# Two Strassen pairs in the second half of the output projection of a hybrid decoder block

## The chip, the cores and the metric

The kernel runs on one core of a Trainium2 chip. The metric is the device time of one execution in microseconds (us). A core has TensorE (PE, with its weight loads listed as PEld), VectorE (DVE), ScalarE (ACT), GpSimd (POOL) and SyncE (SP), which issues most DMA transfers here. The engines run beside each other and wait for each other by semaphores.

## What is computed

One decoder layer on 256 positions of width 2048, all in float32, and a final norm. Cut to what matters:

```python
u = rms_norm(h, norm_mix)
z = u @ w_in                      # 13060 columns, 8192 of them merge gates
gates = sigmoid(gz + b_gate)      # (256, 4, 2048)
mixed = sum(gates[:, n] * (branches[n] @ w_branch[n]) for n in range(4))
h = h + mixed @ w_out             # the output projection: 256x2048 by 2048x2048
v = rms_norm(h, norm_ffn)
h = h + (silu(v @ w_ffn_gate) * (v @ w_ffn_up)) @ w_ffn_down
return rms_norm(h, norm_final)
```

## The kernel before

Every float32 matrix product is made from three matmuls of a reduced-precision type (float32r): each operand is split into a high part, which ScalarE rounds (`act`), and a low part, which VectorE subtracts (`tt`), and high x high, high x low and low x high are added up in PSUM. One such product of a 128x128 block of the stationary side (the activations, transposed) with a 128x512 block of weights is 3 matmuls (`mm3s`).

The large projections run through `pair`: two weight column blocks of 512 columns, `wl` and `wr`, against both halves of the 256 positions, over K in steps of 256 rows, called pairs (`kp`, 8 of them for K = 2048). Four accumulators, q[t][i] (t the half of the positions, i left or right block), fill four PSUM banks for the whole loop; there is one set of them, so the next call of `pair` starts in them when the results of the call before have been read out. A direct pair has its weights in four pieces of 128x1024 altogether: `wpiece` loads two K blocks of one column block into a `raw` slot (four slots), and makes `whi` and `wlo` (four slots each). It takes 8 products, 24 matmuls.

A Strassen pair (`kp in skps`) treats the 2x2 blocks of the stationary side and the 2x2 blocks of the weights as a Winograd-Strassen product: 7 products, 21 matmuls. It needs sums of the weight blocks (`s_weights`: four additions, then high and low parts of the four blocks and of three of the sums) and sums of the stationary blocks (`s_sums`: four subtractions or additions of 128x128, high and low part). Four of its products go into four PSUM banks of their own, p1, p5, p7, p6, which gather over all Strassen pairs of the call, three into q. After the last Strassen pair these banks are joined by ScalarE and VectorE into an SBUF tile `u`, which whoever called `pair` adds to q's results. In the kernel before the gates use Strassen for pairs 0, 3 and 6, the FFN for up to four of eight, the output projection for none.

The output projection is two calls of `pair`, `cc` = 0 and 1, one for each 1024 columns of `w_out`; the second is the half that the change touches. Its stationary side is the merged branches, transposed, in four tiles `mt` (`mh`, `ml`), all of them complete early in the first half. After each half VectorE adds q into `hn` (which holds x), ScalarE sums its squares, and two entries go on the list `later`. The next call of `pair` runs that list when it reaches its third pair (`late["at"]` is 2): `to_T` transposes the 1024 columns of `hn` on TensorE, 16 transposes into four PSUM banks, and ScalarE and VectorE read them out as `vth` and `vtl`, the stationary side of the FFN. For the FFN's Strassen pairs (0, 2, 3, 5) it also makes their sums, by way of a scratch tile `s_temp`. That is one tile, tag `se` with one buffer, taken out of the pool `late["sx"]`, which is `mxp` in this stage. The banks for the transposes come from `bank()`, which goes round the same four PSUM banks p1, p5, p7, p6 in a fixed turn; in the second half its turn is p5, p7, p6, p1.

The order in which each engine executes its instructions is fixed when the program is built. A planner takes the instructions in program order as their rank, and may place a later one earlier on an engine when its inputs and a buffer are there; a call to `keep_in_program_order` forbids that for one instruction. `split=1` holds the last pair back so that q[0] is finished before q[1].

Of the kernel before, what the change touches and what calls it, by code (L numbers as in the profile page):

```python
# [8 lines left out]
F32 = mybir.dt.float32  # L9
F32R = mybir.dt.float32r  # L10
AF = mybir.ActivationFunctionType
ALU = mybir.AluOpType
AX = mybir.AxisListType

P = 128
S = 256
D = 2048
NKT = D // P
# [11 lines left out]
def hybrid_block_kernel(  # L30
# [7 lines left out]
    nc = tc.nc  # L38
# [4 lines left out]
    w_out = w_out[0]  # L43
# [6 lines left out]
    wp = ctx.enter_context(tc.tile_pool(name="wp", bufs=4))  # L50
# [5 lines left out]
    def act(o, i, f=AF.Copy, **kw):  # L56
        return nc.scalar.activation(o, i, f, **kw)  # L57

    def tt(o, a, b, op, eng=None):
        return (eng or nc.vector).tensor_tensor(out=o, in0=a, in1=b, op=op)  # L60
# [9 lines left out]
    late = {"psum": None, "turn": 0, "at": 1}  # L70
# [7 lines left out]
    def rd(t):  # L78
        return t.bitcast(F32)
# [121 lines left out]
    def s_sums(v, sh, sl, w):  # L201

        a11, a21, a12, a22 = v[:, 0, 0:P], v[:, 0, P:S], v[:, 1, 0:P], v[:, 1, P:S]
        tt(w[:, 0, :], a21, a22, ALU.subtract)
        tt(w[:, 1, :], w[:, 0, :], a11, ALU.subtract)
        tt(w[:, 2, :], a11, a21, ALU.subtract)
        tt(w[:, 3, :], a12, w[:, 1, :], ALU.add)
        act(sh, w)
        tt(sl, w, rd(sh), ALU.subtract)

    def s_temp(v_too=True):
        e = late["sx"].tile([P, 3, 512], F32, tag="se", name="s_temp", bufs=1)
        return e[:, 0, :].rearrange("p (a b) -> p a b", a=2), e[:, 1, :].rearrange("p (a b) -> p a b", a=4)

    def mm3s(acc, a, w, first, last, pin=False):

        for x_, w_, st, sp_ in ((a[0], w[0], first, False), (a[0], w[1], False, False), (a[1], w[0], False, last)):
            m = nc.tensor.matmul(acc, x_, w_, start=st, stop=sp_)  # L218
            if pin:
                tc.keep_in_program_order(m)  # L220

    def s_weights(wl, wr, kp):
        sx, nb = late["sx"], late["sx_bufs"]
        rows = slice(kp * 2 * P, (kp + 1) * 2 * P)
        x_ = sx.tile([P, 4, 512], F32, tag="sx", name="sx", bufs=nb)
        nc.sync.dma_start(x_[:, 0:2, :], wr[rows, :].rearrange("(k p) n -> p k n", p=P))
        nc.sync.dma_start(x_[:, 2:4, :], wl[rows, :].rearrange("(k p) n -> p k n", p=P))
        e = sx.tile([P, 3, 512], F32, tag="se", name="se", bufs=1)
        h, lo = (sx.tile([P, 4, 512], F32R, tag=t, name=t, bufs=nb) for t in ("sh", "sl"))
        eh, el = (sx.tile([P, 3, 512], F32R, tag=t, name=t, bufs=nb) for t in ("seh", "sel"))  # L230
        tt(e[:, 0, :], x_[:, 0, :], x_[:, 1, :], ALU.add)
        tt(x_[:, 0, :], x_[:, 0, :], x_[:, 2, :], ALU.add)
        tt(e[:, 1, :], x_[:, 0, :], x_[:, 1, :], ALU.add)
        tt(e[:, 2, :], e[:, 1, :], x_[:, 3, :], ALU.add)
        act(h, x_)
        tt(lo, x_, rd(h), ALU.subtract)
        act(eh, e)
        tt(el, e, rd(eh), ALU.subtract)
        t1, r2, l1, l2 = ((h[:, i, :], lo[:, i, :]) for i in range(4))
        t3, t2, t4 = ((eh[:, i, :], el[:, i, :]) for i in range(3))  # L240
        return l1, l2, r2, t1, t2, t3, t4
# [5 lines left out]
    def pair(wl, wr, nkp, skps, a_of, upool=None, split=0, quiet=False, at_mid=None, order=None, own=False):  # L247

        pq = late["psum"]
        qt = [late["acc"].tile([P, 2, 512], F32, tag=f"q{t}", name=f"q{t}") for t in range(2)]
        q = [[qt[t][:, i, :] for i in range(2)] for t in range(2)]
        p = {}
        ns = len(skps)
        left = {(0, 0): 2 * nkp - ns, (0, 1): 2 * nkp - ns, (1, 0): 2 * nkp - ns, (1, 1): 2 * (nkp - ns),
                1: ns, 5: ns, 6: ns, 7: ns}
        begun = set()
        u = None
        if own:  # L260
            left[1, 0], left[1, 1] = left[1, 0] - 2 * split, left[1, 1] - 2 * split
            left[2, 0] = left[2, 1] = 2 * split
            q = q + [[None, None]]

        def go(i, a, w, pin=False):
            left[i] -= 1
            if i in (1, 5, 6, 7) and i not in begun:
                p[i] = pq.tile([P, 512], F32, tag=f"p{i}", name=f"p{i}")
            if i in ((2, 0), (2, 1)) and i not in begun:
                q[2][i[1]] = pq.tile([P, 512], F32, tag=f"p{(1, 5)[i[1]]}", name="last")  # L270
            mm3s(q[i[0]][i[1]] if isinstance(i, tuple) else p[i], a, w, i not in begun, left[i] == 0, pin)
            begun.add(i)

        held = []
        for n_kp, kp in enumerate(order or range(nkp)):
            if n_kp == late["at"] and (not skps or min(skps) > n_kp) and not quiet:
                run_later()
            blk, sums = a_of(kp, kp in skps)
            if kp in skps:
                l1, l2, r2, t1, t2, t3, t4 = s_weights(wl, wr, kp)  # L280
                go(1, blk(0, 0), l1)
                go(5, sums(0), t1)
                go(7, sums(2), t3)
                go(6, sums(1), t2)
                go((0, 0), blk(1, 0), l2)
                go((0, 1), sums(3), r2)
                go((1, 0), blk(1, 1), t4)
                if kp == max(skps):

                    u = upool.tile([P, 4, 512], F32, tag="u", name="u", bufs=1)  # L290
                    act(u[:, 0, :], p[1])
                    tt(u[:, 1, :], u[:, 0, :], p[6], ALU.add)
                    tt(u[:, 2, :], u[:, 1, :], p[7], ALU.add)
                    tt(u[:, 1:4:2, :], p[5].unsqueeze(1).to_broadcast([P, 2, 512]), u[:, 1:3, :], ALU.subtract)
                    if at_mid is not None:
                        at_mid(u)
                    run_later()
                continue
            rows = slice(kp * 2 * P, (kp + 1) * 2 * P)
            ws = [wpiece(w[rows, :], 2, 512) for w in (wl, wr)]  # L300
            todo = [((t, i), [(blk(j, t), (ws[i][0][:, j, :], ws[i][1][:, j, :])) for j in range(2)])
                    for t in range(2) for i in range(2)]
            if kp >= nkp - split:
                held.append(todo)
                continue
            for i, prods in todo:
                for a, w in prods:
                    go(i, a, w)
        for n in range(4):
            for todo in held:  # L310
                i, prods = todo[n]
                if own and i[0] == 1:
                    i = (2, i[1])
                for a, w in prods:
                    go(i, a, w, pin=True)
        return (qt + [q[2]] if own else qt), u
# [27 lines left out]
    gp = gx.enter_context(tc.tile_pool(name="gp", bufs=2, side="right"))  # L344
# [44 lines left out]
    for kt in range(NKT):  # L389
        hi, lo = wpiece(w_in[kt * P:(kt + 1) * P, C_CF:C_CF + W_CF], 1, W_CF, pin=True)  # L390
# [10 lines left out]
        if kt % 4 in (1, 2):  # L401
            junk = ap_.tile([P, 512], F32, tag="junk", name="junk")
            q, t = kt // 4, kt % 4 - 1
# [22 lines left out]
    for wt, src in ((wab, lru_wa), (wxb, lru_wx)):  # L426
        nc.gpsimd.memset(wt, 0.0)
        v = src[0].rearrange("(j two) c d -> two c j d", two=2)
# [35 lines left out]
    ms = small.tile([P, 2], F32, name="ms", bufs=1)  # L464
# [311 lines left out]
    for n, c in ((1, 0), (1, 1), (3, 0), (3, 1)):  # L776
        if n == 1:
            mixed_of[c] = gp.tile([P, 2, 512], F32, tag="mixed", name="mixed")
        mixed = mixed_of[c]
        col = n * D + c * 512  # L780
        bb = gp.tile([P, 512], F32, tag="bb", name="bb")
        nc.gpsimd.dma_start(bb, b_gate[0, col:col + 512].partition_broadcast(P))
        ag = chunk(w_in[:, C_GZ + col:C_GZ + col + 512], uth, utl, NKT)
        gate = gp.tile([P, 2, 512], F32, tag="gate", name="gate")
# [17 lines left out]
    mp = gx.enter_context(tc.tile_pool(name="mp", bufs=1, side="right"))  # L802
# [54 lines left out]
    def m_of(kp, s):  # L857
        return a_tiles(*mt[kp // 4])(kp % 4, s)
# [18 lines left out]
    def sumsq(dst, src, n):  # L877
        junk = fp.tile([P, 4, 512], F32, tag="u", name="junk2").rearrange("p a b -> p (a b)")[:, :n]
        act(junk, src, AF.Square, accum_out=dst)

    late["at"] = 2
    for cc in range(2):
        cs = slice(cc * 1024, (cc + 1) * 1024)
        nc.sync.dma_start(hn[:, :, cs], x[:, cs].rearrange("(t p) n -> p t n", p=P))
        q, _ = pair(w_out[:, cc * 1024:cc * 1024 + 512], w_out[:, cc * 1024 + 512:(cc + 1) * 1024], NKT // 2, (),
                    m_of if cc else m_split, split=1)
        for t in range(2):
            o = hn[:, t, cs].rearrange("p (a b) -> p a b", a=2)
            tt(o, o, q[t], ALU.add)
            sumsq(ss2[:, t, cc:cc + 1], hn[:, t, cs], 1024)  # L890
        for c in (2 * cc, 2 * cc + 1):
            later.append(lambda c=c: to_T(hn[:, :, c * 512:(c + 1) * 512], vth, vtl, 4 * c, also=(FS, vsh, vsl),
                                          gcol=lambda i: gffn[:, 4 * c + i:4 * c + i + 1]))
    s3.close()
    gx.close()
    rstd2 = const.tile([P, 2], F32, name="rstd2")
# [59 lines left out]
    for cc in range(2):  # L956
        cs = slice(cc * 1024, (cc + 1) * 1024)
        def at_mid(u):
            for t in range(2):
                o = hn[:, t, cs].rearrange("p (a b) -> p a b", a=2)  # L960
                stt(o, u[:, 2 * t:2 * t + 2, :], rstd2[:, t:t + 1], o, ALU.mult, ALU.add)
# [68 lines left out]
```

## Time and profile before

| | us |
|---|---|
| median of three runs | 1507.44 |
| lowest and highest | 1506.28, 1512.24 |
| the profiled execution, its own time | 1510.63 |
| its span, first to last instruction | 1508.4 |
| busy in the span: PE | 1489.2 |
| PEld | 1225.8 |
| DVE | 1202.4 |
| ACT | 821.2 |
| POOL | 71.7 |

The profile is of one execution. Times in it count from the start of its span. A row of the groups view gives the code line, the engine, the operation, the output tile and its inputs, the shape, the number of instructions, their busy time, the mean in ns of one and the idle time of the engine before them. L60 is the helper `tt`, L57 the helper `act`, L120 the weight load in `wpiece`, L165 the transposes and L218 the matmuls of `mm3s`.

### The profile page before, as it was taken

The page shows a single profiled execution, that of the slowest core. Times are in us where ns is not written, and L with a number is a line of the kernel's source. Part 1 is how long each engine was busy: PE and PEld are TensorE (multiplying, and loading weights), DVE is VectorE, ACT ScalarE, POOL GpSimd, SP SyncE. Part 2 cuts the span into 40 slices and gives each one's busy share as a digit, 9 for nine tenths or more (in the row PEclk, how much of TensorE's full clock was granted, in tenths as well). Part 3 has the DMA queues.
Part 4 walks back from the last instruction along what each step waited for, and adds up shares of the span by engine and source line. Part 5 has one row for each costly group of instructions (what it writes and reads, how often), then busy time and mean ns, then how long its engine had stood idle before and what let it go on. Part 6 is the DMA issues. An engine that isn't in the chain of part 4 may idle for free.

```text
span 1508.4 us, 18519 instructions
## 1 busy us (share of the span) xinstructions
PE 1489.2 (99%) x6763; PEld 1225.8 (81%) x6763; DVE 1202.4 (80%) x1400; ACT 821.2 (54%) x944; POOL 71.7 (5%) x94
## 2 busy tenths in 40 slices
PE   8999999999999999999999999999999999999997
PEld 7778888888788888887888888888888888888885
DVE  4756755678898889887568899999989899897865
ACT  5544844555554555544456555555555555655643
POOL 3000300001000000000000000000000000001000
PEclk9999999999999999999999999999999999999999
DMA  7645455556666676656557666576657568786663
GB/s 239 211 150 160 133 187 163 160 187 226 209 210 198 220 261 199 209 191 209 186 180 251 218 216 220 197 237 201 234 179 237 189 223 279 254 279 223 205 213 115
DMA packets 158603, 311.54 MB, mean 207 GB/s; under 512 B 10608, under 2 KB 12720, under 8 KB 158384
## 3 DMA queue, kind: packets, MB, share of 16 engines
q1 hardware_dynamic: 154528, 297.87, 60.4%
q0 software_dynamic: 3952, 12.49, 2.4%
q8 instruction: 53, 0.87, 0.2%
q14 instruction: 38, 0.31, 0.1%
q10 hardware_dynamic: 32, 0.01, 0.0%
HBM read 301.41 MB, written 8.91 MB: 206 GB/s over the span
## 4 chain that ended last, share of the span: by engine, by line
PE 96%; DVE 1%; DMA 1%; issue 1%; ACT 0%; SPq 0%; POOLq 0%; POOL 0%; ACTq 0%; DVEq 0%
PE q L218 61%; PE acc L133 20%; PE p L218 11%; PE ps L165 2%; DMA xq<-in_x_dram 0%; DVE wlo L60 0%; DMA raw<-in_w_in_dram 0%; PE ps L541 0%; PE ps L737 0%; PE ps L560 0%; PE ps L499 0%; ACT whi L57 0%; PE ps L607 0%; PE ps L754 0%; PE ps L693 0%
## 5 line engine op out<-in xcount | busy, mean ns | idle before, releaser
L60 DVE TENSOR_TENSOR wlo<-raw,whi 128x1024 fp32r<-128x1024 f32 (+1 forms) x412 | 504.3, 1230 | 188.7 <-ACT whi L57 186.0
L57 ACT ACTIVATE whi<-raw 128x1024 fp32r<-128x1024 f32 (+1 forms) x412 | 431.7, 1050 | 393.4 <-PE q L218 166.0
L57 ACT ACTIVATE sh<-sx 128x2048 fp32r<-128x2048 f32 x62 | 118.8, 1916 | 116.6 <-PE q L218 41.8
L133 PE MATMUL acc<-wlo,uth 128*128 128x512 f32 (+1 forms) x448 | 173.9, 391 | 0.0
L133 PE MATMUL acc<-whi,utl 128*128 128x512 f32 (+1 forms) x448 | 173.8, 389 | 0.0
L60 DVE TENSOR_TENSOR sl<-sx,sh 128x2048 fp32r<-128x2048 f32 x62 | 141.9, 2289 | 36.1 <-ACT sh L57 36.0
L133 PE MATMUL acc<-whi,uth 128*128 128x512 f32 (+1 forms) x448 | 167.6, 390 | 0.6 <-DVE nat L64 0.4
L218 PE MATMUL q<-wlo,vth 128*128 128x512 f32 x424 | 165.8, 391 | 0.0
L218 PE MATMUL q<-whi,vtl 128*128 128x512 f32 x424 | 165.6, 391 | 0.0
L218 PE MATMUL q<-whi,vth 128*128 128x512 f32 x424 | 164.5, 391 | 0.0
L218 PE MATMUL q<-whi,ah 128*128 128x512 f32 x512 | 159.5, 389 | 0.0
L218 PEld LDWEIGHTS q<-whi,ah 128*128 128x128 f32 x512 | 96.1, 188 | 19.9
L60 DVE TENSOR_TENSOR sel<-se,seh 128x1536 fp32r<-128x1536 f32 x62 | 108.6, 1751 | 4.5 <-ACT seh L57 4.1
L57 ACT ACTIVATE seh<-se 128x1536 fp32r<-128x1536 f32 x62 | 91.7, 1479 | 22.3 <-PE q L218 20.3
L218 PE MATMUL q<-wlo,ah 128*128 128x512 f32 x256 | 99.8, 390 | 0.3 <-DVE wlo L60 0.3
L133 PEld LDWEIGHTS acc<-wlo,uth 128*128 128x128 f32 x448 | 84.8, 189 | 16.9 <-issue 1.0
L133 PEld LDWEIGHTS acc<-whi,utl 128*128 128x128 f32 x448 | 84.8, 189 | 16.5 <-issue 0.7
L133 PEld LDWEIGHTS acc<-whi,uth 128*128 128x128 f32 x448 | 81.7, 188 | 16.9 <-issue 0.7
L218 PE MATMUL q<-wlo,uth 128*128 128x512 f32 x240 | 93.8, 391 | 0.0
L218 PE MATMUL q<-whi,uth 128*128 128x512 f32 x240 | 93.8, 391 | 0.0
L218 PE MATMUL q<-whi,utl 128*128 128x512 f32 x240 | 93.5, 389 | 0.0
L60 DVE TENSOR_TENSOR se<-sx 128x512 f32<-128x512 f32 x124 | 86.2, 695 | 8.8 <-DMA sx<-in_w_in_dram 7.4
(393 smaller groups left out, 2535.6 us busy)
## 6 DMA issues: line engine op xcount, KB each, us to landing
raw<-in_w_in_dram SPq DMA_DIRECT2D x156, 512.0 KB, 3.4
raw<-in_w_ffn_down_dram SPq DMA_DIRECT2D x70, 512.0 KB, 5.1
raw<-in_w_ffn_gate_dram SPq DMA_DIRECT2D x53, 512.0 KB, 4.1
raw<-in_w_ffn_up_dram SPq DMA_DIRECT2D x53, 512.0 KB, 4.8
sx<-in_w_in_dram SPq DMA_DIRECT2D x36, 512.0 KB, 4.3
sx<-in_w_ffn_up_dram SPq DMA_DIRECT2D x35, 512.0 KB, 3.7
sx<-in_w_ffn_gate_dram SPq DMA_DIRECT2D x35, 512.0 KB, 4.7
raw<-in_w_branch_dram SPq DMA_DIRECT2D x32, 512.0 KB, 4.4
```

The lines of the kernel that those rows point to most:

```text
L57: return nc.scalar.activation(o, i, f, **kw)
L60: return (eng or nc.vector).tensor_tensor(out=o, in0=a, in1=b, op=op)
L133: m = nc.tensor.matmul(acc, x_, w_, start=st, stop=sp_)
L165: m = nc.tensor.transpose(pt[:, i * S + t * P:i * S + (t + 1) * P], nat[:, t, (c0 + i) * P:(c0 + i + 1) * P], ident)
L218: m = nc.tensor.matmul(acc, x_, w_, start=st, stop=sp_)
```

## The change

In the second half of the output projection pairs 3 and 6 become Strassen pairs. Their weight operands are made by a new function, `s_weights_spare`, in tiles of tags that the gate stage has left over: the two weight loads in `raw` slots, the three sums in `se`, the high parts of the four blocks in the gates' `u` tile, the low parts in the two `mixed` tiles, high and low parts of two sums in the two `gate` tiles, and of the third sum in `bb2`. `m_sums` makes the sums of the stationary side, from `mh` + `ml` in `s_temp`, with high and low part in the two `bb` tiles. For both halves `pair` is given a pool for `u` and a function `at_mid`, which adds `u` into `hn` right after the last Strassen pair; in the first half there is none, so it isn't called there.

```diff
+    def s_weights_spare(wl, wr, kp):
+        rows = slice(kp * 2 * P, (kp + 1) * 2 * P)
+        r, l_ = (wp.tile([P, 2, 512], F32, tag="raw", name="raw", bufs=4) for _ in range(2))
+        nc.sync.dma_start(r, wr[rows, :].rearrange("(k p) n -> p k n", p=P))
+        nc.sync.dma_start(l_, wl[rows, :].rearrange("(k p) n -> p k n", p=P))
+        e = late["sx"].tile([P, 3, 512], F32, tag="se", name="se", bufs=1)
+        h = mp.tile([P, 4, 512], F32R, tag="u", name="sh", bufs=1)
+        lo_r, lo_l = (gp.tile([P, 2, 512], F32R, tag="mixed", name="sl") for _ in range(2))
+        eh, el = (gp.tile([P, 2, 512], F32R, tag="gate", name="se2") for _ in range(2))
+        e2 = mp.tile([P, 2, 512], F32R, tag="bb2", name="se3")
+        tt(e[:, 0, :], r[:, 0, :], r[:, 1, :], ALU.add)
+        tt(r[:, 0, :], r[:, 0, :], l_[:, 0, :], ALU.add)
+        tt(e[:, 1, :], r[:, 0, :], r[:, 1, :], ALU.add)
+        tt(e[:, 2, :], e[:, 1, :], l_[:, 1, :], ALU.add)
+        for src, hi, lo in ((l_, h[:, 2:4, :], lo_l), (r, h[:, 0:2, :], lo_r), (e[:, 0:2, :], eh, el),
+                            (e[:, 2, :], e2[:, 0, :], e2[:, 1, :])):
+            act(hi, src)
+            tt(lo, src, rd(hi), ALU.subtract)
+        t1, r2 = ((h[:, i, :], lo_r[:, i, :]) for i in range(2))
+        l1, l2 = ((h[:, 2 + i, :], lo_l[:, i, :]) for i in range(2))
+        t3, t2 = ((eh[:, i, :], el[:, i, :]) for i in range(2))
+        return l1, l2, r2, t1, t2, t3, (e2[:, 0, :], e2[:, 1, :])
...
-                l1, l2, r2, t1, t2, t3, t4 = s_weights(wl, wr, kp)
+                l1, l2, r2, t1, t2, t3, t4 = late.get("weights", s_weights)(wl, wr, kp)
...
+    def m_sums(kp, s):
+        blk, _ = m_of(kp, s)
+        if not s:
+            return blk, None
+        v, w = s_temp()
+        mh, ml = (t[:, 2 * (kp % 4):2 * (kp % 4) + 2, :] for t in mt[kp // 4])
+        tt(v, rd(mh), rd(ml), ALU.add)
+        sh, sl = (gp.tile([P, 4, P], F32R, tag="bb", name="ms") for _ in range(2))
+        s_sums(v, sh, sl, w)
+        return blk, lambda i: (sh[:, i, :], sl[:, i, :])
+
     late["at"] = 2
+    late["weights"] = s_weights_spare
     for cc in range(2):
...
-        q, _ = pair(w_out[:, cc * 1024:cc * 1024 + 512], w_out[:, cc * 1024 + 512:(cc + 1) * 1024], NKT // 2, (),
-                    m_of if cc else m_split, split=1)
+        def at_mid(u):
+            for t in range(2):
+                o = hn[:, t, cs].rearrange("p (a b) -> p a b", a=2)
+                tt(o, o, u[:, 2 * t:2 * t + 2, :], ALU.add)
+
+        q, _ = pair(w_out[:, cc * 1024:cc * 1024 + 512], w_out[:, cc * 1024 + 512:(cc + 1) * 1024], NKT // 2, (3, 6) if cc else (),
+                    m_sums if cc else m_split, fp, split=1, at_mid=at_mid)
...
+    del late["weights"]
```

## Rows read from the trace of the kernel before

**Rows 1.** The page, part 1 (busy us, share, instructions) and part 4 (chain by engine).

```profile
PE 1489.2 (99%) x6763; PEld 1225.8 (81%) x6763; DVE 1202.4 (80%) x1400; ACT 821.2 (54%) x944; POOL 71.7 (5%) x94
...
PE 96%; DVE 1%; DMA 1%; issue 1%; ACT 0%; SPq 0%; POOLq 0%; POOL 0%; ACTq 0%; DVEq 0%
```

**Rows 2.** Windows: from:to, length, busy us and instructions per engine, clock, DMA share.

```profile
749.70:796.10 46.40, 46.40 (x209) 37.62 (x209) 29.23 (x42) 26.08 (x38) 0.00 (x0) 1.00 0.58 181
...
567.70:612.50 44.80, 44.80 (x198) 36.70 (x197) 42.17 (x42) 23.57 (x21) 0.54 (x1) 1.00 0.65 210
...
702.10:746.90 44.80, 43.97 (x197) 35.79 (x198) 25.01 (x27) 17.57 (x19) 0.00 (x0) 1.00 0.67 224
...
749.70:757.00 7.30, 7.30 (x35) 5.91 (x35) 3.22 (x3) 3.85 (x6) 0.00 (x0) 1.00 0.53 165
```

**Rows 3.** Waits of PE: who waited for whom, us in total, times, longest.

```profile
PE q L218 <- ACT whi L57: 1.2, 1, 1.2
```

**Rows 4.** The chain in order of time: start us, us, what and how many.

```profile
762.63 36.34 PE q L218 x156
...
925.76 4.99 PE p L218 x22
```

**Rows 5.** Timeline of PE, the second half: start us, us, engine, line, operation.

```profile
761.16 1.47 PE L165 MATMUL ps<-ident,hn 128*128 128x128 f32 x12
...
796.06 0.39 PE L218 MATMUL q<-whi,vth 128*128 128x512 f32 x1
```

**Rows 6.** Groups of VectorE, 378 to 700 us, then the changed half.

```profile
L60 DVE TENSOR_TENSOR se<-sx 128x512 f32<-128x512 f32 x34 | 24.5, 720 | 7.8 <-DMA sx<-in_w_in_dram 7.4
...
L60 DVE TENSOR_TENSOR u<-u,p 128x512 f32<-128x512 f32 x12 | 8.2, 687 | 2.1 <-PE p L218 1.9
L60 DVE TENSOR_TENSOR u<-p,u 128x1024 f32<-128x1024 f32 x6 | 7.3, 1224 | 0.2
...
L60 DVE TENSOR_TENSOR wlo<-raw,whi 128x1024 fp32r<-128x1024 f32 x17 | 20.8, 1223 | 17.1 <-ACT whi L57 17.1
...
L60 DVE TENSOR_TENSOR s_temp<-s_temp 128x128 f32<-128x128 f32 x12 | 3.1, 282 | 0.0
...
L60 DVE TENSOR_TENSOR vsl<-s_temp,vsh 128x512 fp32r<-128x512 f32 x3 | 2.1, 692 | 0.9 <-ACT vsh L57 0.9
```

**Rows 7.** Groups of ScalarE, 378 to 700 us.

```profile
L57 ACT ACTIVATE whi<-raw 128x1024 fp32r<-128x1024 f32 x85 | 89.9, 1061 | 66.4 <-PE q L218 45.0 <-issue 20.1 <-DMA raw<-in_w_in_dram 1.1
...
L57 ACT ACTIVATE u<-p 128x512 f32<-128x512 f32 x6 | 3.5, 579 | 0.0
```

**Rows 8.** Timeline of VectorE in the second half.

```profile
757.08 1.23 DVE L60 TENSOR_TENSOR wlo<-raw,whi 128x1024 fp32r<-128x1024 f32 x1 [4.16 <-ACT whi L57]
...
777.04 0.48 DVE L68 SCALAR_TENSOR_TENSOR vtl<-ps,prm,vth 128x256 fp32r<-128x256 f32 x1
777.82 0.69 DVE L60 TENSOR_TENSOR vsl<-s_temp,vsh 128x512 fp32r<-128x512 f32 x1 [0.30 <-ACT vsh L57]
...
793.47 1.22 DVE L60 TENSOR_TENSOR hn<-hn,q 128x1024 f32<-128x1024 f32 x1 [0.48 <-PE q L218]
```

**Rows 9.** Timeline of ScalarE: first and third use of the scratch tile.

```profile
762.32 0.82 ACT L57 ACTIVATE s_temp<-ps,prm 128x256 f32<-128x256 f32 x2
...
773.43 0.82 ACT L57 ACTIVATE s_temp<-ps,prm 128x256 f32<-128x256 f32 x2
```

**Rows 10.** Timeline of SP: the weight loads of pairs 3 and 6.

```profile
750.68 0.37 SPq L120 DMA_DIRECT2D raw<-in_w_out_dram  x1
752.95 0.37 SPq L120 DMA_DIRECT2D raw<-in_w_out_dram  x1
...
769.26 0.37 SPq L120 DMA_DIRECT2D raw<-in_w_out_dram  x1
771.39 0.37 SPq L120 DMA_DIRECT2D raw<-in_w_out_dram  x1
```

**Rows 11.** DMA issues: count, KB each, median us to landing.

```profile
raw<-in_w_out_dram SPq DMA_DIRECT2D x32, 512.0 KB, 4.6
```

## Prediction

> **What bounds the kernel now.** I read the page first: TensorE is busy 1489.2 us of a span of 1508.4, and 96% of the chain that ended last is TensorE [rows 1]. Then the windows: in the stretch of the changed half, 749.7 to 796.1 us, PE is busy 46.40 of 46.40 us at a granted clock of 1.00 (the full 2.4 GHz), VectorE 29.23, ScalarE 26.08 [rows 2]. So PE sets the end, and only fewer or faster matmuls shorten this stretch; any new PE wait lengthens it one for one. The same view shows how far VectorE can be loaded before PE waits: 42.17 of 44.8 us (94%) in a stretch of the gates, with PE still full. In the list of PE's waits the longest one of the matmuls of `pair` is a single wait of 1.2 us for ScalarE's high part of a weight piece [rows 3]. Last the chain in order of time: in this half 156 matmuls take 36.34 us, 0.233 us each [rows 4]. The half's matmuls have no gap between the transposes at 761.16 and the first FFN matmul at 796.06 [rows 5].
>
> **What the change takes away.** A direct pair costs 8 products of 3 matmuls (24), a Strassen pair 7 products (21). Two pairs: 6 matmuls at 0.233 us = **-1.40 us**, all on the path. The Strassen matmuls use other tiles; at the pace of the Strassen matmuls of the FFN (22 in 4.99 us, 0.227 each [rows 4]) 42 of them would give another 42 x 0.006 = 0.26 us. I take 0.233 and keep 0.26 for the low end. The Trainium skill, page "TensorE: Matmul & The Clock Gate", section "Back-to-back issue gap", gives 518 cycles for N = 512 at full clock, 216 ns, and for a sustained stream of weight load and matmul about 131 ns; by these figures the saving is estimated at 1.30 or 0.79 us. The measured 0.233 us decides.
>
> **What it adds on VectorE.** Per Strassen pair, with the means of [rows 6] (where the same size isn't there, the nearest): four sums of 128x512 at 0.72 = 2.88; three low parts of 128x1024 at 1.22 = 3.67; one low part of 128x512 at 0.69; together 7.24 us for the weight operands. The sums of the stationary side: one add 0.72, four 128x128 operations at 0.28 = 1.13, one low part 0.69, together 2.54. Of this a direct pair's two `wlo` (2.45) fall away. Net 9.78 - 2.45 = 7.33, twice 14.7. The joining of the products into `u`: 2 x 0.69 + 1.22 = 2.60; `at_mid`: 2 x 1.22 = 2.44. Total **+19.7 us of VectorE** in a stretch that becomes 45.0 us long and in which 29.23 are taken: 48.9. That doesn't fit. At the 94% shown above 42.4 fit, so some 6.5 us must move out. There is room: the half before uses 25.01 of 44.8 us [rows 2], and the sums of pair 3 (2.54) need only `mt`, finished long before; and in the stretch itself VectorE works ahead on the first two FFN pairs (4 x 1.22 = 4.9), which may be done later. So the work fits only with nearly all of the lead spent. ScalarE gets per pair 3 x 1.06 + 2 x about 0.58 - 2 x 1.06, or 2.2, and once the copy into `u`, 0.58 [rows 7]: 5 us on 26, which lies beside PE. DMA moves the same 512 KB pieces, no DMA is added or removed, but the two `raw` slots of a Strassen pair are held for 7.2 us of VectorE work instead of 2.5, so SP's next loads wait that much longer, with later pieces queued behind them.
>
> **Where PE may wait.** By the matmul pace, pair 2 starts at 762.46 and pair 3 at 768.06 (5.60 us each); with the saving pair 4 starts at 772.96, pair 6 at 784.16, pair 7 at 789.06, and the half ends at 794.66.
> (a) Pair 3. Its pieces are issued at 750.68 and 752.95 and land 4.6 us later, 757.6 [rows 10, 11]. VectorE does pair 2's pieces from 757.08 [rows 8]; 2.5 + 7.24 us later, at 766.8, all operands are there: no wait, if this work runs ahead of the evacuation of the transposed `hn`. The four product banks are a second condition: `bank()` hands them to the 16 transposes in the order p5, p7, p6, p1, and the last is read out only at 777.5 [rows 8]. The first product goes into p1. Bounds: 0, if the evacuation (no hurry before) is done by 768 or the q products go first; 777.5 - 768.06 = 9.4 if nothing moves. The nearer row is that of the ScalarE copies into `s_temp`, 762.32 to 773.43 [rows 9], three uses through one `se` tile with weight pieces between them that have time. I take 1.0.
> (b) Pair 6. Its `raw` loads are issued at 769.26 and 771.39, in slots freed by pair 4 [rows 10], land at 776.0; `sh`, `sl` and the sums are single and come free when pair 3's products are done, 773 to 776. Then 2.54 + 7.24 gives 786 to 788. PE begins at 784.16 with the products whose operands are ready, and needs the last operand 18 matmuls (4.2 us) later, 788.4. Bounds 0 to 4; I take 0.5.
> (c) The first FFN pair. It starts in the accumulator q[0], which is free when `hn` has taken it up; the addition stands at 793.47 now, 2.6 us before the end [rows 8]. Now `u` and `at_mid` come ahead of it, behind pair 6's last product (about 787): 0.58 + 2.60 + 2.43 + 1.22 = 6.8, so 793.8, against 794.66. It is clean if nothing else of VectorE stands between; two weight pieces there (2.45) make it 1.6 late. Bounds 0 to 2; I take 0.5.
> Sum: -1.40 + 1.0 + 0.5 + 0.5 = **+0.6 us**. The profiled execution took 1510.63 us by its own time (span 1508.4, 2.2 around it); it is 3.2 above the median of the three runs, 1507.44. A difference of +0.6 on the median gives **1508.0 us**.
>
> **The rivals.**
> Clean: the order of VectorE's work puts the Strassen operands ahead of what has time, and the stalls are 0. For it: no PE wait in the gate stage, which has Strassen pairs 0, 3 and 6 with the same single tiles. Against it: there VectorE carries no transposes of `hn`. -1.40, so 1506.0 us.
> VectorE-bound: p1 holds pair 3 until 777.5, PE first does the 9 q matmuls of pair 3 and 6 of pair 4 (3.5 us), 5.9 are left; with 1.0 at (b) and (c), -1.4 + 6.9 = +5.5, 1513 us.
> Slower: pair 3's four sums are written in the one tile `se`, which the three `s_temp` uses of the transposes and the sums of pair 3 share. They come earlier in the program; should the tile be given out in that order, the third use ends with `vsl` at 778.5 [rows 8]. Then 2.88 for the four sums and 1.06 + 1.22 for the high and low part of the right weights: 783.7. Only the first product, the l2 product and the free ones of pair 4 (12 matmuls, 2.8 us) can precede it, so of the 15.6 us from 768.06 to 783.7 PE stands 12.8; -1.4 makes +11.4, 1519 us. The bound of 7.5 us is passed when `se` comes free after 774.6. For it: the three uses do run one after another now. Against it: VectorE idles from 753 to 757 (3.22 busy of 7.3 us [rows 2]) while pair 3's weights are landing, and these sums need nothing else. The Trainium skill, page "PSUM — Partial Sum Buffer", section "Engine vs sequencer instructions", says that matmuls start and complete in program order; by that rule a late operand holds everything queued behind it, which is this rival. The wait of 1.2 us [rows 3] shows such a stop, and no row here shows one being passed.
> That the change does less than it says (one pair only) would be 0.7 us and is inside the forecast's range.
>
> **How the numbers follow.** Forecast (stalls of 0.7 to 4.4 in sum): 0.45, 1508.0 us. Clean: 0.32, 1506.0. VectorE-bound: 0.14, 1513. Slower by the tile: 0.09, 1519. The range reaches from the clean case with the faster pace and a run or two below the median (1506.0 - 0.3 - 0.6) to just above the VectorE-bound case: 1505.1 to 1514. A measurement of this kernel can tell some 0.5% (7.5 us) from no change. Faster by that much nothing here can give: 0.01. Slower: the tile's case and the tail of the VectorE-bound one, 0.10. Within 0.5%: 0.89.
>
> **What would show it.** In the profile after: 6 matmuls fewer in the half, 24 matmuls into `p` banks; VectorE busy 94% or more from 757 to 795; PE waits named for `sl`, `se` or `sh` of VectorE and ScalarE before pair 3 and pair 6, and for `hn` at the first FFN matmul. Clean is shown by a first FFN matmul at 794.7 and no such waits. The slower rival is shown by the first sum of pair 3 standing behind the third `vsl`. The prediction is wrong if the stretch ends more than 2 us before or more than 4 us behind 796.06, or if the stages around it change their length.

## The result, and the profile after

The changed kernel takes 1528.02 us (median of 4 runs, 1525.69 to 1529.78), the kernel before in the same count of runs 1509.84 (1506.28 to 1514.51). The ratio is 1.0116, 95% interval 1.0101 to 1.0131: slower by about 17.5 us (the medians lie 18.2 apart), outside the range of 1505.1 to 1514.

The page of the changed kernel: part 1, then the slices of PE and of its granted clock (40 slices of 38.2 us, tenths), then the chain by engine (part 4).

```profile
PE 1493.3 (98%) x6757; PEld 1228.3 (80%) x6757; DVE 1221.4 (80%) x1429; ACT 826.1 (54%) x951; POOL 72.4 (5%) x94
...
PE   8999999999999999999969999999999999999997
...
PEclk9999999999999999999979999999999999999999
...
PE 94%; DVE 2%; DMA 1%; ACT 1%; issue 1%; SPq 0%; POOLq 0%; POOL 0%; ACTq 0%; DVEq 0%
```

The six matmuls are gone (6763 in [rows 1], 6757 here), and VectorE is busy 19.0 us longer, as the sum of its instructions said (19.7). But one slice of PE shows a 6, and its clock a 7: that slice is 764 to 802 us, in the changed half. The list of PE's waits names what stands there; the first line is the largest wait of the whole run.

```profile
PE p L218 <- DVE vtl L68: 9.2, 1, 9.2
PE p L218 <- ACT sh L57: 4.9, 1, 4.9
...
PE q L218 <- DVE hn L60: 0.3, 1, 0.3
```

Both large waits are of products into the `p` banks, of pair 3. The timeline of PE there (start us, us, engine, line, operation, and in brackets the idle time before it and who ended it):

```profile
772.00 0.39 PE L218 MATMUL q<-sh,ml 128*128 128x512 f32 x1
781.57 0.77 PE L218 MATMUL p<-sh,mh 128*128 128x512 f32 x1 [9.19 <-DVE vtl L68]
...
788.07 0.79 PE L218 MATMUL p<-sh,ms 128*128 128x512 f32 x1 [4.88 <-ACT sh L57]
...
793.45 0.44 PE L218 MATMUL q<-whi,mh 128*128 128x512 f32 x1
793.73 0.39 PE L218 MATMUL q<-wlo,mh 128*128 128x512 f32 x1
```

The first line is the last thing that PE could do of pair 3 without a bank or a sum, the l2 product. Then it stands for the last read-out of bank p1, which the transposes had used, and again for the sums of pair 3. VectorE's timeline says why they come so late:

```profile
762.08 1.23 DVE L60 TENSOR_TENSOR sl<-raw,sh 128x1024 fp32r<-128x1024 f32 x1 [0.30 <-ACT sh L57]
...
771.48 0.68 DVE L60 TENSOR_TENSOR vsl<-s_temp,vsh 128x512 fp32r<-128x512 f32 x1
...
777.95 0.69 DVE L60 TENSOR_TENSOR vsl<-s_temp,vsh 128x512 fp32r<-128x512 f32 x1 [0.30 <-ACT vsh L57]
...
780.94 0.48 DVE L68 SCALAR_TENSOR_TENSOR vtl<-ps,prm,vth 128x256 fp32r<-128x256 f32 x1
781.61 0.69 DVE L60 TENSOR_TENSOR vsl<-s_temp,vsh 128x512 fp32r<-128x512 f32 x1 [0.19 <-ACT vsh L57]
782.34 0.69 DVE L60 TENSOR_TENSOR s_temp<-mh,ml 128x512 f32<-128x512 f32 x1
...
784.78 0.69 DVE L60 TENSOR_TENSOR ms<-s_temp,ms 128x512 fp32r<-128x512 f32 x1 [0.69 <-ACT ms L57]
785.51 0.69 DVE L60 TENSOR_TENSOR se<-raw 128x512 f32<-128x512 f32 x1
```

The low part of the left weights, which needs no scratch tile, is made at 762.08, 9 us ahead of its use. Then the one tile `se` goes through five uses end to end: the three of the transposes (each ends with a `vsl`), at 782.34 the sums of pair 3's stationary side, at 785.51 its weight sums. `mh` and `ml`, the only inputs of the fourth use, had been ready for 90 us (since 692).

The sum of the loss. From the twelve transposes to the first FFN matmul it is 34.9 us in [rows 5], and 764.62 to 816.23, or 51.6, after: 16.7 longer. The waits give 9.2 + 4.9 + 0.3 = 14.4. From the first wait on PE's clock falls, and behind it PE runs at half clock, as the windows show (from:to, length, busy us and instructions of PE, PEld, DVE, ACT, POOL, clock, DMA share, GB/s):

```profile
760.00:771.00 11.00, 11.00 (x55) 9.10 (x54) 7.76 (x12) 7.00 (x12) 0.00 (x0) 1.00 0.43 142
772.30:781.50 9.20, 0.08 (x1) 0.00 (x0) 6.77 (x15) 6.05 (x12) 0.00 (x0) 0.73 0.53 166
781.50:786.00 4.50, 1.62 (x3) 0.83 (x3) 3.55 (x8) 0.71 (x2) 0.00 (x0) 0.50 0.00 0
786.00:793.40 7.40, 5.33 (x12) 3.97 (x13) 6.83 (x12) 3.52 (x4) 0.00 (x0) 0.50 0.43 120
793.40:800.00 6.60, 6.60 (x29) 5.31 (x28) 3.30 (x4) 1.42 (x3) 0.00 (x0) 0.99 0.07 27
```

The 12 matmuls from 788.07 to 793.45 take 5.4 us, where 12 x 0.233 would be 2.8, and the three at 781.57 lose some 0.6 more: 3.2 us. With the saving of 1.4 that makes 14.4 + 3.2 - 1.4 = 16.2 of the 16.7; the other 0.5 has no row of its own. The profiled execution of after (1529.78 us, span 1528.1) also reaches the half 3.5 us later than that of before, in code that wasn't changed. At the program's start alone its waits for `xq` and `dqn` are 1.5 us longer (3.5 and 1.9 against 2.9 and 1.0); where the rest lies isn't shown.

### The profile page after: what moved, and what is told of

It reads as the page before. It is cut to its first block, busy times and chain, and to the rows that moved or that the text cites. A ratio compares the mean times of both kernels' runs of the same rounds, so it can differ in the third digit from the quotient of the medians.

```text
span 1528.1 us, 18549 instructions
## 1 busy us (share of the span) xinstructions
PE 1493.3 (98%) x6757; PEld 1228.3 (80%) x6757; DVE 1221.4 (80%) x1429; ACT 826.1 (54%) x951; POOL 72.4 (5%) x94
## 4 chain that ended last, share of the span: by engine, by line
PE 94%; DVE 2%; DMA 1%; ACT 1%; issue 1%; SPq 0%; POOLq 0%; POOL 0%; ACTq 0%; DVEq 0%
PE q L218 59%; PE acc L133 20%; PE p L218 11%; PE ps L165 2%; DVE wlo L60 1%; DMA raw<-in_w_out_dram 1%; ACT whi L57 0%; DMA xq<-in_x_dram 0%; DMA raw<-in_w_in_dram 0%; PE ps L565 0%; PE ps L761 0%; PE ps L584 0%; PE ps L523 0%; PE ps L631 0%; DVE s_temp L60 0%
## 5 line engine op out<-in xcount | busy, mean ns | idle before, releaser
L60 DVE TENSOR_TENSOR sl<-sx,sh 128x2048 fp32r<-128x2048 f32 x62 | 141.9, 2289 | 35.1 <-ACT sh L57 34.9
L218 PEld LDWEIGHTS q<-whi,vth 128*128 128x128 f32 x424 | 79.6, 188 | 16.9 <-ACT whi L57 0.7
```

## The experiments

The theory at the start (A): the single scratch tile is given out in program order, so pair 3's sums stand behind the transposes. Its rivals: (B) the product bank p1, which the transposes read out last, is the cause; (C) VectorE has more work than the half holds. Each edit is against the changed kernel if nothing else is said; "before" is the median of the kernel before, measured beside it on the same chip, 1510.47 for the first four, 1510.87 for the next four, 1510.40 for the last four.

**A tile of their own for the sums of pairs 3 and 6.**

```diff
-        e = late["sx"].tile([P, 3, 512], F32, tag="se", name="se", bufs=1)
+        e = late["sx"].tile([P, 3, 512], F32, tag="se4", name="se", bufs=1)
...
-        v, w = s_temp()
+        e = late["sx"].tile([P, 3, 512], F32, tag="se4", name="s_temp4", bufs=1)
+        v, w = e[:, 0, :].rearrange("p (a b) -> p a b", a=2), e[:, 1, :].rearrange("p (a b) -> p a b", a=4)
```

> Only change against the changed kernel: the sums of pairs 3 and 6, of the weights and of the stationary side, get a scratch tile of their own (6 KB more per partition), so they no longer share the one tile with the transposes of hn. Theory A (that shared tile orders pair 3's sums behind the three uses by the transposes): the 4.9 us wait of the p products for sh goes, the sums of the stationary side move ahead by some 20 us or more, but p1 is still read out last, so the 9.2 us wait for vtl stays at 7 to 9; time 1521 to 1524. Theory B (only the product bank p1 counts, and VectorE was free to do the sums any time): the 4.9 stays in some form and the time is that of the changed kernel, about 1528. Theory C (VectorE is full): the same amount of work, so 1526 to 1528.

Measured: 1517.26 us, ratio to before 1.004 (1.0027 to 1.0054). Some 11 of the 17.5 us are gone, more than A expected. The first use of the new tile, in VectorE's timeline, stands in the stage before the projection; then PE's waits:

```profile
689.76 0.68 DVE L60 TENSOR_TENSOR s_temp<-mh,ml 128x512 f32<-128x512 f32 x1
```

```profile
PE p L218 <- DVE vtl L68: 3.0, 1, 3.0
...
PE p L218 <- ACT sh L57: 1.1, 1, 1.1
```

Pair 3's stationary sums move from 782 to 690. The wait for the bank shrinks too, which A didn't expect: with the sums there, the three products of pair 3 that go into q run at 767.9, the direct pairs after them, and the products into p1 stand behind those. There, at 786.39, they still wait 3.0 us for the bank; the 1.1 is pair 6's.

**The turn of the PSUM banks moved on, so that p1 is read out first.**

```diff
     for cc in range(2):
+        if cc:
+            late["turn"] = (late["turn"] + 3) % 4
```

> Only change against the changed kernel: the turn of the four PSUM banks is moved on by three before the second half, so that the transposes of hn use p1 first and p6 last. Theory A (the shared scratch tile): p1's product can go at once, but the next one still waits for the sums, until the same moment; the wait of 9.2 us turns into one wait of 13 to 14 us, named for ScalarE or VectorE and the sums; time within 1.5 of the changed kernel, about 1527. Theory B (the bank): the 9.2 us go, and with them the time at half clock; 1514 to 1517. Theory C: about 1527.

Measured: 1526.52 us, 1.0104 (1.0085 to 1.0123). PE's timeline has one wait instead of two:

```profile
783.89 0.79 PE L218 MATMUL p<-sh,ms 128*128 128x512 f32 x1 [14.85 <-ACT sh L57]
```

As A said, the bank only held the same products a second time: with it out of the way they wait for the sums, 14.9 us. B by itself falls.

**Both edits together.**

> Both edits together: scratch of their own for pairs 3 and 6, and p1 first in the turn. Theory A and B together (each alone leaves PE standing at the other): no PE wait over 2 us in the half, no stretch at half clock, time 1508 to 1512, with before at 1509. Theory C (19.7 us more of VectorE don't fit): waits of 5 us or more remain, named for VectorE, time 1515 or more.

Measured: 1518.18 us, 1.005 (1.0032 to 1.0067), the same as the own tile alone, and not the 1508 to 1512 of A and B together. The two waits that are left:

```profile
788.02 0.94 PE L218 MATMUL p<-se,ms 128*128 128x512 f32 x3 [3.07 <-DVE vtl L68]
...
792.71 0.80 PE L218 MATMUL p<-sh,ms 128*128 128x512 f32 x1 [3.75 <-ACT sh L57]
```

The first is again a bank that the transposes read out late (now p6), the second is pair 6. C had 1515 or more, with waits of 5 us or more named for VectorE; by its time alone it couldn't be ruled out here.

**The list of transposes behind pair 6.**

```diff
-                    m_sums if cc else m_split, fp, split=1, at_mid=at_mid)
+                    m_sums if cc else m_split, fp, split=1, at_mid=at_mid, quiet=cc == 1)
```

> Only change against the changed kernel: in the second half the list of transposes of hn runs after pair 6 instead of ahead of pair 2, so that it comes behind both Strassen pairs in program order. Theory A and B (the transposes hold the scratch tile and the banks): pairs 3 and 6 run without waits; the transposes are read out beside pair 7 and the start of the FFN, at a price of 0 to 5 us there; time 1508 to 1513. Theory C: VectorE has the same work up to the FFN, waits of 5 us or more remain, 1515 or more.

Measured: 1514.19 us, 1.0023 (1.0013 to 1.0032). No wait at pair 3 or 6; the largest ones stand at the start of the FFN, for the read-out of the transposes:

```profile
796.95 0.50 PE L218 MATMUL q<-whi,vth 128*128 128x512 f32 x1 [1.67 <-ACT vth L57]
800.00 0.66 PE L165 MATMUL ps<-ident,hn 128*128 128x128 f32 x4 [0.99 <-DVE vtl L68]
```

The time lies a little above the expected 1508 to 1513. The same VectorE work without the large waits speaks against C.

**Pair 3 alone, and pair 6 alone.**

```diff
-        q, _ = pair(..., NKT // 2, (3, 6) if cc else (),
+        q, _ = pair(..., NKT // 2, (3,) if cc else (),
```

In the second kernel the tuple is `(6,)`.

> Only pair 3 is a Strassen pair, all else as in the changed kernel. If the loss sits at pair 3 (its sums and its first product bank behind the transposes of hn): both waits of PE, 9.2 and 4.9 us, stay, 3 matmuls more than in the changed kernel; time 1525 to 1528 beside 1510 of before. If much of the loss is pair 6's or VectorE's load as a whole: VectorE has some 7 us less to do, time 1516 to 1521.

> Only pair 6 is a Strassen pair, all else as in the changed kernel. If the order behind the transposes is the cause: pair 6's sums come behind the three uses of the scratch tile too, but those end at 778.5 by the trace of before, the sums then take until about 787, and pair 6 is due at 785; a wait of 0 to 3 us, time 1509 to 1513. If Strassen operands in these tiles cost the loss wherever they stand: half of it, 1517 to 1520.

Measured: pair 3 alone 1527.94 us, 1.0116 (1.0101 to 1.0131), the whole loss with the same two waits:

```profile
782.29 0.77 PE L218 MATMUL p<-sh,mh 128*128 128x512 f32 x1 [9.19 <-DVE vtl L68]
...
788.80 0.80 PE L218 MATMUL p<-sh,ms 128*128 128x512 f32 x1 [4.89 <-ACT sh L57]
```

Pair 6's VectorE work (7.3 us) isn't needed for the loss, which speaks against C once more. Pair 6 alone: 1516.55 us, 1.004 (1.0025 to 1.0055), between the two expectations, with a wait that was put at 0 to 3:

```profile
789.41 0.80 PE L218 MATMUL p<-sh,ms 128*128 128x512 f32 x1 [5.63 <-ACT sh L57]
```

Its sums come behind the third use of the scratch tile too (778.61, after a `vsl` that starts at 776.03), and then they are delayed in the queues: ScalarE's part of them (`ms`) stands behind weight pieces whose loads haven't landed.

```profile
779.13 1.06 ACT L57 ACTIVATE whi<-raw 128x1024 fp32r<-128x1024 f32 x1 [1.70 <-DMA raw<-in_w_out_dram]
782.57 1.06 ACT L57 ACTIVATE whi<-raw 128x1024 fp32r<-128x1024 f32 x1 [2.37 <-DMA raw<-in_w_ffn_gate_dram]
783.53 0.61 ACT L57 ACTIVATE ms<-s_temp 128x512 fp32r<-128x512 f32 x1
```

**No new tile, only the order: pair 3's operands written ahead of the transposes.**

```diff
+        if cc:
+            early = m_sums(3, True), s_weights_spare(w_out[:, 1024:1536], w_out[:, 1536:], 3)
         q, _ = pair(...
```

Pair 3 then takes what `early` holds.

> No tile more than the changed kernel has: the sums and the weight operands of pair 3 are written into the program ahead of the second call of pair, and so ahead of the three uses of the scratch tile by the transposes. If the scratch tile is given out in program order and that is the cause: pair 3's sums move ahead to before 760, the wait for sh goes, that for vtl shrinks to 3 or less; time 1512 to 1518, as with a tile of its own. If it was the added room that helped there, not the order: 1524 or more.

Measured: 1517.1 us, 1.0041 (1.0026 to 1.0055). The only large wait is pair 6's:

```profile
791.79 0.80 PE L218 MATMUL p<-sh,ms 128*128 128x512 f32 x1 [3.65 <-ACT sh L57]
```

VectorE now makes pair 3's stationary sums ahead of the transposes:

```profile
692.06 0.68 DVE L60 TENSOR_TENSOR s_temp<-mh,ml 128x512 f32<-128x512 f32 x1
```

No memory was added, PE has no wait at pair 3, and the time is that of the own tile (1517.26). So order, not room, is what the own tile changed.

**The list of transposes behind pair 6, and slots of their own for the Strassen pairs' loads.**

```diff
-        r, l_ = (wp.tile([P, 2, 512], F32, tag="raw", name="raw", bufs=4) for _ in range(2))
+        r, l_ = (late["sx"].tile([P, 2, 512], F32, tag="raw4", name="raw4", bufs=2) for _ in range(2))
```

> The list of transposes behind pair 6, as in e4_list_late, and in addition two slots of their own for the weight loads of the Strassen pairs (8 KB more per partition), so that pairs 4, 5 and 7 keep their four raw slots. If what e4_list_late still loses (some 3 us against before) comes from weight loads that start late: 1508 to 1511. If it comes from the read-out of the transposes beside the FFN's first pairs and a full VectorE: unchanged, 1513 to 1515, with the waits of PE at the start of the FFN as before.

Measured: 1512.16 us, 1.001 (1.0000 to 1.0019), 1.3 above before. Some 2 us of what e4_list_late lost are gone with the added slots; the intervals of the two ratios overlap, so the share of the loads is indicated, not settled. PE's waits beyond those of before are three of 0.6 us, the first for `hn`, the others for `vth` and `vtl`:

```profile
795.28 0.50 PE L218 MATMUL q<-whi,vth 128*128 128x512 f32 x1 [0.61 <-DVE hn L60]
...
797.60 0.50 PE L218 MATMUL q<-whi,vth 128*128 128x512 f32 x1 [0.56 <-ACT vth L57]
...
799.40 0.50 PE L218 MATMUL q<-whi,vtl 128*128 128x512 f32 x1 [0.59 <-DVE vtl L68]
```

**Two buffers for the shared scratch tile.**

```diff
-        e = late["sx"].tile([P, 3, 512], F32, tag="se", name="s_temp", bufs=1)
+        e = late["sx"].tile([P, 3, 512], F32, tag="se", name="s_temp", bufs=late.get("two", 1))
...
+    late["two"] = 2
```

`late["two"]` is set for the output projection alone, and the line of the weight sums' `e` in `s_weights_spare` gets the same `bufs`.

> Only change against the changed kernel: the scratch tile of the second half has two buffers instead of one (6 KB more, as in e1_own_scratch), still shared by the transposes of hn and the Strassen pairs. If its buffers are given out in program order: pair 3's stationary sums are the fourth use and wait for the second, its weight sums are the fifth and wait for the third; the wait for sh goes nearly (under 2 us of 4.9), the one for vtl shrinks since the three uses overlap (4 to 7 of 9.2); time 1517 to 1523, between e1_own_scratch and the changed kernel. If only room counts, not order: as e1_own_scratch, 1517, with pair 3's stationary sums made in the first half.

Measured: 1522.85 us, 1.0082 (1.0068 to 1.0096). The same 6 KB as in the first experiment gain somewhat under half as much (5 of the 17.5 us, against 11). VectorE's timeline shows the buffers going round in program order:

```profile
773.36 0.69 DVE L60 TENSOR_TENSOR vsl<-s_temp,vsh 128x512 fp32r<-128x512 f32 x1
774.76 0.68 DVE L60 TENSOR_TENSOR s_temp<-mh,ml 128x512 f32<-128x512 f32 x1
778.47 0.69 DVE L60 TENSOR_TENSOR vsl<-s_temp,vsh 128x512 fp32r<-128x512 f32 x1 [0.17 <-ACT vsh L57]
779.68 0.68 DVE L60 TENSOR_TENSOR se<-raw 128x512 f32<-128x512 f32 x1
```

The fourth use begins after the second has ended (774.05), the fifth after the third (779.16). The wait for the bank is 6.3 us, within the 4 to 7; that for `sh` is 3.8 and was put under 2.

**Pair 6 alone with a tile of its own.** The edit of the first experiment and the tuple `(6,)`.

> Pair 6 alone as a Strassen pair, with a scratch tile of its own. In e6_only6, without that tile, PE waited 5.6 us for sh. If the order in the shared tile causes that: no wait over 1 us, time 1509 to 1512, the same as before. If it is the late weight loads and VectorE's queue: a wait of 3 us or more stays, 1514 to 1517.

Measured: 1510.94 us, 1.0001 (0.9992 to 1.0010). The 5.6 us wait is gone, no wait that before hadn't is over 0.5 us. The saving of one pair, 0.7 us, can't be seen at this interval (1.2 us faster to 1.5 slower).

**Pairs 0 and 3, and pairs 0, 3 and 6, as in e9_late_room.**

```diff
-        q, _ = pair(..., NKT // 2, (3, 6) if cc else (),
+        q, _ = pair(..., NKT // 2, (0, 3) if cc else (),
```

In the second kernel the tuple is `(0, 3, 6)`.

> As e9_late_room (list of transposes behind the last Strassen pair, own slots for the weight loads), but Strassen pairs 0 and 3 instead of 3 and 6, so that the transposes are read out beside pairs 4 to 7 and not beside the FFN's first pairs. If e9_late_room's remaining 1 to 2 us lie in that read-out: the waits at the start of the FFN go, time 1508.5 to 1511, 1.4 below before at best. If VectorE's amount of work is the limit: waits of 2 us or more somewhere in the half, 1512 to 1515.

> As e9_late_room with a third Strassen pair, 0. The order theory has nothing against it: pair 0's operands are made in the first half, where VectorE is busy 25 of 45 us; 0.7 us less than e9_late_room, 1510.5 to 1513. If VectorE's amount is the limit, the 9.8 - 2.5 = 7.3 us more cost 2 to 6 us: 1514 to 1518.

Measured: pairs 0 and 3 1508.55 us against 1510.40, 0.9985 (0.9976 to 0.9994): faster than both kernels, and than the one before by some 2 us (0.15%), where the matmuls removed say 1.4; the interval (0.9 to 3.6 us) holds that. PE has no wait in the half that before didn't have. Windows of the half and of the one before it, then two rows of VectorE's timeline:

```profile
749.70:795.00 45.30, 45.30 (x205) 36.87 (x204) 37.76 (x54) 28.18 (x43) 0.00 (x0) 1.00 0.50 151
702.00:747.00 45.00, 44.58 (x200) 36.28 (x201) 31.49 (x39) 20.16 (x23) 0.00 (x0) 1.00 0.73 245
```

```profile
686.73 0.68 DVE L60 TENSOR_TENSOR s_temp<-mh,ml 128x512 f32<-128x512 f32 x1
...
699.29 0.69 DVE L60 TENSOR_TENSOR se<-raw 128x512 f32<-128x512 f32 x1
```

Pair 0's operands are made from 687 on, some 60 us ahead of their use, and VectorE does 31.5 us in the half before, not the 25.0 of [rows 2]. The transposes stand at 771 to 774, with pairs 4 to 7 behind them to cover the read-out. The third pair gains nothing: 1511.56 us, 1.0013 (1.0004 to 1.0022). With pair 6 last, the transposes move to 788 and the waits at the start of the FFN come back:

```profile
PE ps L165 <- DVE vtl L68: 1.0, 1, 1.0
...
PE q L218 <- DVE hn L60: 0.4, 1, 0.4
```

Its trace also has a wait of 1.2 us for `u` at 440 us, in the gate stage, where the kernel before has none and the other runs 0 to 0.8; so not all that the third pair fails to gain is the transposes'.

## Why the prediction was wrong, step by step

**The bound and the saving held, the price of a wait did not.** PE sets the end, and six matmuls at 0.233 us are 1.4 us; e12_pairs03, which adds no wait, is faster by 0.9 to 3.6 us, which holds that gain. But a wait didn't go into the time one for one, as the prediction had it: 14.4 us of waits cost 17.6, the half clock behind them included.

**The amount of VectorE work was right, the conclusion "that doesn't fit" was not the cause.** Busy time rose by 19.0 us against 19.7 in the sum. The same work in e9_late_room and e12_pairs03 costs PE 1.8 us of waits and none; there VectorE is busy 32.5 and 31.5 us in the half before, which takes part of the work, as the prediction said that it could. Nor was VectorE full where PE stood: of the 9.2 us from 772.3 in the changed kernel it is busy 6.77, and from 760.5 to 798.5 (the stretch for which the prediction named 94% as the sign) 27.95 of 38.00, 74%. So the VectorE-bound rival falls.

**Step (a) failed.** It had the two locks (the sums behind the evacuation, the bank p1 last) and their bound, 9.4 us, and then took 1.0, because the weight pieces between the uses of `se` had time. But the order wasn't made by what had time. Measured at this place, where the step took 1.0: 9.2 + 4.9 us of waits, past its bound too, and 3.2 of half clock. The reason written against the rival called slower, that VectorE idles from 753 to 757 and these sums need nothing else, is the step that misled: they need the tile `se`. Its five uses run in program order, and neither an idle VectorE nor inputs ready 90 us ahead moved the fourth one forward; it moved to 690 and 692 as soon as the tile (e1_own_scratch) or the order of the program (e7_early) allowed it.

**The slower rival, with a chance of 0.09, is what happened.** Its sign was as described: the first weight sum of pair 3 behind the third `vsl` (785.51 after 782.30). Its page, the Trainium skill's "PSUM — Partial Sum Buffer", section "Engine vs sequencer instructions", has matmuls start in program order; the trace agrees, nothing passed the product that stood for 9.19 us. Its price was 12.8 us of standing still; measured are 14.1, and 3.2 of half clock on top, which it didn't have. Within the 14.1 three terms were mis-sized: the stationary sums of pair 3 use the tile between the third `vsl` and the weight sums (3.1 us more, 782.34 to 785.47); of the weight operands only two sums and a high part precede the product (785.51 to 788.07, 2.6 us, not 5.2); and PE had 6 matmuls to do in that time, not 12 (1.4 us more). Together that gives 14.7; the 0.6 above the measured 14.1 is the slower pace of the three matmuls between the two waits, which stands in the 3.2.

**Step (b)** put 0 to 4 us on pair 6 and took 0.5. In the changed kernel nothing shows, since pair 3 has delayed everything. By itself pair 6 waits 5.6 us (e6_only6), above the bound: the step counted the single operand tiles, but not the scratch tile, nor the weight pieces that stand ahead of `ms` in ScalarE's queue and wait for their loads.

**Step (c)** was 0.5 and measured 0.3 for `hn`.

**What would have shown it in the trace of before:** the three uses of `s_temp` there start at 762.32, 767.88 and 773.43, each only after the `vsl` of the one before it. Rows of VectorE and ScalarE:

```profile
766.39 0.69 DVE L60 TENSOR_TENSOR vsl<-s_temp,vsh 128x512 fp32r<-128x512 f32 x1 [0.30 <-ACT vsh L57]
...
767.88 0.82 ACT L57 ACTIVATE s_temp<-ps,prm 128x256 f32<-128x256 f32 x2
...
772.27 0.69 DVE L60 TENSOR_TENSOR vsl<-s_temp,vsh 128x512 fp32r<-128x512 f32 x1 [0.30 <-ACT vsh L57]
```

To add a fourth and a fifth use to the same tile behind these in program order is to start them at 778.5 at the earliest, even where an engine idles.

## What to carry to other kernels

When a change borrows tiles, list for each of them the uses that come ahead in program order and when the last one ends; where the tile has one buffer, that time is a lower bound for the new work, and an idle engine or a ready input doesn't lift it. A saving on the engine that sets the end is worth having only where its operands can be made ahead: two Strassen pairs (3 and 6) cost 17.5 us with their sums behind the transposes, and two (0 and 3) gained some 2 with the transposes behind them and load slots of their own. If two conditions hold the same instruction, undoing one of them can show nothing (e2_turn), so undo each one alone and both together.

## What the runs showed of the hardware

After PE had stood for 9.2 us the granted clock in the windows is 0.50, the 1.2 GHz level, and stays there through a second wait of 4.9 us until 793.4; matmuls of 512 columns step at 0.43 us there, 0.233 us before and after. The half clock added 3.2 us to 14.1 us of waiting. In e12_pairs03 the 12 matmuls of pair 3 into the `p` banks step at 0.2275 us (2.73 us from 765.05), and its 9 into q at the same pace; in the same half those of the direct pairs, also into q, step at 0.233, and in the FFN (880 to 960 us) direct ones at 0.227 too. This is the faster pace that the prediction kept for its low end (0.26 us); why it is faster, no run tells.
